# Projections of a decoder trunk: the products of two blocks in one sequence, instead of one block after the other

## The chip, the cores and the metric

The kernel runs on one core of one Trainium2 chip. The metric is the device time of one execution in microseconds. The median of three runs before the change is 2873.17 us, between 2871.62 and 2875.73. One more execution was profiled; its trace is what is read here.

## The reference

The reference is a decoder trunk of two layers (`DEPTH = 2`), with one sequence of 256 tokens, a width of 2048 and 256 memory tokens, all in float32:

```python
def reference(x, mem, ...):
    mem_n = rms_norm(mem, mem_norm_g)
    for l in range(DEPTH):
        hn = rms_norm(x, mix_norm_g[l])
        if l % 2 == 0:
            x = x + even_mixer(hn, ...)      # gated conformer convolution and differential attention
        else:
            x = x + odd_mixer(hn, ...)       # b * causal_conv3(c * u), then a projection
        x = x + cross_attention(rms_norm(x, xattn_norm_g[l]), mem_n, xq_w[l], xk_w[l], xv_w[l], xo_w[l])
        x = x + sq_relu_mlp(rms_norm(x, mlp_norm_g[l]), mlp_w1[l], mlp_w2[l])
    return rms_norm(x, final_norm_g)
```

What matters here are the dense projections with 2048 inputs: `even_w_in` (values and gates of the convolution, q, k, v of 8 differential heads), `even_w_out`, `odd_w_in`, `odd_w_out`, and for each layer `xq`, `xk`, `xv`, `xo` of a cross attention with 4 heads of 512. The convolution of the even layer has 31 taps, and the cross attention's scores are `q k^T / sqrt(512)` with a softmax over the memory.

## The kernel before, in words

**A product in two parts.** Activations lie with channels on the 128 partitions and the 256 tokens along a row. Each float32 number is split into a hi part (rounded to the matmul's fp32r type) and a lo part (what is left). An activation chunk of 128 channels holds hi and lo side by side, 512 columns (`act.both`); `act.hi` is the first half. A block is 128 output channels; its weights are 2048 x 128, loaded as two tiles of 128 x 1024 (eight chunks of inputs each). `weights` (L178) loads one such tile (`raw`), casts it to `whi` on ACT (L189), and makes `wlo` as the difference on DVE (L190). For each of the 16 chunks there is one hi product, 512 columns wide, weights hi times activations hi and lo, and one lo product, 256 columns, weights lo times activations hi. All 32 add up in one PSUM bank of 512 columns (`ps_mm`, four banks), whose halves `summed` (L235) adds: a copy on ACT, an addition on DVE.

**Buffers.** The pools rotate: four `raw` tiles, three `whi` tiles (L71), four `wlo` tiles (L184). A tile is written again when its last reader is done.

**The order of the products.** `proj` (L232, by `proj_group` and `wide_piece`) does a block as 8 hi, 8 lo, 7 hi, 8 lo, 1 hi. `proj_long` (L227) does 15 hi, 16 lo, 1 hi. `proj_rows` (values, rows of tokens) is another form and not touched. `proj` is used for q, k, convolution values and gates, for the keys of layer 0 and the queries of both layers; `proj_long` for the output projections, the input projection of the odd layer and the keys of layer 1.

**What sets the order of other work.** Each call of `weights` first runs what is due by a counter of such calls (L179 to L181): convolution taps from a list, `rate[0]` of them per call (one in the heads, three in the gated channels and behind them), and stages of attention whose delay has passed. In the even layer eight differential heads and eight gated channels alternate in four groups of two heads and two channels; the scores of a head (`sc`, L431) are due two calls after its k block. In cross attention the scores of a head (`sx`, L682) are due one call after its fourth query block (L736), their transposes (`ptx`) one call and the outputs (`pox`) one more behind. Matmuls stand in the order of the program where `strict` is set; loads, `wlo` and taps have orders of their own among themselves; the rest on ACT and DVE is put in order by the scheduler, and each engine then takes its list from the front.

**The MLP** (`Chunk`, `Step`, L760 on), more than half of the span, has its own order and isn't touched.

Of the kernel before, what the change touches and what calls it, by code (L numbers as in the profile page):

```python
# [10 lines left out]
F32 = mybir.dt.float32  # L11
# [3 lines left out]
ALU = mybir.AluOpType  # L15
AX = mybir.AxisListType

P = 128
D = 2048
S = 256  # L20
NC = D // P
# [24 lines left out]
def trunk(ctx: ExitStack, tc: tile.TileContext, d):  # L46
# [184 lines left out]

    def proj(src, act):  # L232
        return proj_group([src], act)[0]

    def summed(ps):  # L235

        t = tmp32("sum")
        A.copy(t, ps[:, S:])
        V.tensor_tensor(t, ps[:, :S], t, op=ALU.add)
        return t  # L240
# [138 lines left out]
    def even_mixer():  # L379
# [40 lines left out]

        def qk(c, hl, name, sign):
            t = summed(proj(w[2 * NA + c], xa))
# [88 lines left out]
        def head(h):  # L511
            mem_piece(m, mss, h)
            if h == H1 - 1:
                stage(4, mem_rows)
            qkt = pools["att"].tile([P, 2, 2, S], F32R, tag="pt", name="dqk")
            q, k = qk(h, qkt[:, 0], "dq", -0.125), qk(H1 + h, qkt[:, 1], "dk", 1.0)
            stage(D0, lambda h=h, q=q, k=k: scores(h, q, k))
# [5 lines left out]
        def gated(c):  # L523
            av = summed(proj(w[c], xa))
            V.tensor_tensor(av, av, r, op=ALU.mult)
            ag = summed(proj(w[NA + c], xa))
            V.tensor_tensor(ag, ag, r, op=ALU.mult)
# [81 lines left out]
        for c, ps in enumerate(proj_group([d["even_out"][c] for c in range(3)], cat, (1, 0))):  # L609
            residual(c, ps, nxt, nss, "xat0")  # L610
        for c in range(3, NC):
            residual(c, proj_long(d["even_out"][c], cat), nxt, nss, "xat0")
        return nxt, nss, kmem


    def odd_mixer(xa, ss):
        w = d["odd_in"]
        y, m = Act(NC, "y"), Act(NC, "mem")
        begun = [NC, 2 * NC, 0, NC + 1]
        made = dict(zip(begun, proj_group([w[c] for c in begun], xa, (1, 0))))  # L620
        r = rstd(ss.acc, D, ss.rows)
        for c in range(NC):
            if c % 2:
                mem_piece(m, None, c // 2)
            cc = summed(made.pop(NC + c) if NC + c in made else proj_long(w[NC + c], xa))
            V.tensor_tensor(cc, cc, r, op=ALU.mult)
            uu = summed(made.pop(2 * NC + c) if 2 * NC + c in made else proj_long(w[2 * NC + c], xa))
            V.tensor_tensor(uu, uu, r, op=ALU.mult)
# [7 lines left out]
            bb = summed(made.pop(c) if c in made else proj_long(w[c], xa))  # L636
            V.tensor_tensor(bb, bb, r, op=ALU.mult)
# [3 lines left out]
        nxt, nss = Act(NC, "xn"), SumSq()  # L641
        for c in range(NC):
            residual(c, proj_long(d["odd_out"][c], y), nxt, nss, "xat1")
        return nxt, nss, kmem
# [31 lines left out]
    def cross(l, xa, ss, kmem):  # L676
# [64 lines left out]
        strict[0] = False  # L741
        for c in range(4, NC):
            residual(c, proj_long(d[f"xo{l}"][c], oa), nxt, nss, f"mlp{l}")
        return nxt, nss
# [488 lines left out]
```

## Time and profile before

| | |
|---|---|
| median of three runs | 2873.17 us |
| profiled execution | 2874.36 us |
| its span, first to last instruction | 2872.2 us |
| mean granted TensorE clock | 0.998 |
| PE busy | 2853.1 us (99%), 15871 matmuls |
| DVE busy | 2258.0 us (79%) |
| ACT busy | 1635.1 us (57%) |
| read from memory | 535.13 MB, 187 GB/s over the span |

How to read it: busy time is what the engine's own instructions took. Matmuls overlap, so a group's sum is more than its time on the engine; the distance from one start to the next is what a matmul costs. In the timeline a row gives the start, the time from the first start to the last end, the engine, the line (most lines are those of helpers: L169 records matmuls, L59 all of ACT and DVE), the operation, out<-in by the program's names, the shapes and the count of instructions merged. A bracket at the end of a row is idle time of that engine just before it, and what ended it. The even layer lies at 0 to 530 us, its cross attention at 530 to 736, its MLP behind it up to 1430; the odd layer's mixer at 1430 to 1965, its cross attention at 1965 to 2170, and the last MLP behind that.

### The profile page before, as it was taken

The numbers are of one execution on the slowest core, as the hardware profiler recorded it, in microseconds if no ns is written. First come the engines' busy times: TensorE is split into PE (matmuls) and PEld (weight loads), VectorE is DVE, ScalarE is ACT, GpSimd is POOL, SyncE is SP. The second block draws the span as 40 slices with busy tenths as digits, with TensorE's granted clock in tenths as the row PEclk, the third lists the DMA queues.
The fourth block names the chain that finished last, engine by engine and source line by source line (L and its number), as shares of the span: only waits on it lengthen the run. The fifth ranks groups of instructions, "written<-read, shape, count | busy, mean of one in ns | idle before, by whom it ended". The sixth has DMA issues, their size and how long they took to land.

```text
span 2872.2 us, 42098 instructions
## 1 busy us (share of the span) xinstructions
PE 2853.1 (99%) x15871; PEld 2484.0 (86%) x15871; DVE 2258.0 (79%) x3489; ACT 1635.1 (57%) x2290; POOL 65.8 (2%) x92
## 2 busy tenths in 40 slices
PE   9999999999999999999999999999999999999998
PEld 7888888898888888888888888888988888888886
DVE  7899987767788888888887765467677888888888
ACT  6665445555565665656654444455555656656565
POOL 0000000000000000000000000000000000000000
PEclk9999999999999999999999999999999999999999
DMA  7455565545686776967666665655456867869675
GB/s 246 159 187 169 183 198 189 171 150 178 199 250 199 219 236 199 265 195 235 192 200 196 196 202 189 194 190 168 152 180 195 252 208 216 232 202 266 191 239 166
DMA packets 210060, 578.27 MB, mean 201 GB/s; under 512 B 17856, under 2 KB 83520, under 8 KB 209856
## 3 DMA queue, kind: packets, MB, share of 16 engines
q1 hardware_dynamic: 199344, 537.30, 57.6%
q0 software_dynamic: 10512, 38.28, 6.8%
q8 instruction: 125, 2.05, 0.3%
q14 instruction: 79, 0.65, 0.1%
HBM read 535.13 MB, written 2.10 MB: 187 GB/s over the span
## 4 chain that ended last, share of the span: by engine, by line
PE 84%; DVE 10%; ACT 3%; DMA 2%; issue 1%; SPq 0%; DVEq 0%; ACTq 0%; POOLq 0%; POOL 0%
PE mm L169 66%; PE p L169 8%; PE mmr L169 7%; DVE wlo L59 3%; DVE cv L59 2%; DVE tw L59 1%; ACT whi L59 1%; DVE raws L59 1%; DVE x L59 1%; PE sx L169 1%; PE pox L169 1%; DMA wlo<-raw 1%; DMA raw<-even_in 1%; DVE sum L59 1%; ACT tw L59 1%
## 5 line engine op out<-in xcount | busy, mean ns | idle before, releaser
L59 ACT CAST whi<-raw 128x1024 fp32r<-128x1024 f32 (+1 forms) x881 | 923.8, 1051 | 465.1 <-PE mm L169 309.5
L59 DVE TENSOR_TENSOR wlo<-raw,whi 128x1024 fp32r<-128x1024 f32 (+1 forms) x808 | 981.8, 1220 | 143.1 <-ACT whi L59 132.7
L169 PE MATMUL mm<-xn,whi 128*128 128x512 f32 x3840 | 938.0, 392 | 0.6 <-DVE xn L59 0.6
L169 PEld LDWEIGHTS mm<-xn,whi 128*128 128x128 f32 x3840 | 702.5, 189 | 133.0 <-DVE xn L59 0.8
L169 PEld LDWEIGHTS mm<-xn,wlo 128*128 128x128 f32 x3840 | 501.2, 191 | 24.0 <-DVE wlo L59 0.2
L169 PE MATMUL mm<-xn,wlo 128*128 128x256 f32 x3840 | 509.5, 283 | 0.0
L59 ACT COPY sum<-mm 128x256 f32<-128x256 f32 x272 | 101.0, 372 | 426.5 <-PE mm L169 424.9
L59 DVE TENSOR_TENSOR sum<-mm,sum 128x256 f32<-128x256 f32 x272 | 114.4, 421 | 183.5 <-ACT sum L59 183.2
L169 PE MATMUL mm<-hid,whi 128*128 128x512 f32 x1024 | 254.9, 391 | 0.0
L169 PEld LDWEIGHTS mm<-hid,whi 128*128 128x128 f32 x1024 | 192.7, 188 | 39.7
L59 ACT CAST tw<-raws 128x1024 fp32r<-128x1024 f32 x128 | 128.5, 1046 | 130.9 <-DVE raws L59 128.8
L59 DVE TENSOR_TENSOR raws<-raws 128x512 f32<-128x512 f32 x256 | 176.5, 689 | 6.0
L59 DVE TENSOR_TENSOR x<-x,mm 128x256 f32<-128x256 f32 x256 | 107.4, 420 | 90.8 <-PE mm L169 86.1
L59 DVE TENSOR_TENSOR tw<-raws,tw 128x1024 fp32r<-128x1024 f32 x128 | 151.8, 1222 | 26.4 <-ACT tw L59 26.2
L169 PE MATMUL p<-tw,hs 128*128 128x512 f32 x576 | 154.3, 394 | 0.7 <-DVE tw L59 0.7
L169 PE MATMUL mmr<-whi,mem 128*128 128x512 f32 x512 | 137.4, 390 | 0.0
L169 PEld LDWEIGHTS mm<-hid,wlo 128*128 128x128 f32 x1024 | 131.0, 191 | 6.4 <-DMA wlo<-raw 1.8
L169 PE MATMUL mm<-hid,wlo 128*128 128x256 f32 x1024 | 133.2, 283 | 0.3 <-DMA wlo<-raw 0.2
L169 PEld LDWEIGHTS p<-tw,hs 128*128 128x128 f32 x576 | 108.1, 188 | 26.3 <-DVE tw L59 1.6
L169 PE MATMUL mm<-mem,whi 128*128 128x512 f32 x512 | 126.3, 393 | 0.0
L169 PE MATMUL mm<-o,whi 128*128 128x512 f32 x512 | 124.7, 392 | 0.0
L786 POOL DMA_DIRECT2D wlo<-raw x73 | 62.1, 852 | 2587.2 <-ACT wlo L59 2213.9
(204 smaller groups left out, 3152.3 us busy)
## 6 DMA issues: line engine op xcount, KB each, us to landing
raw<-w SPq DMA_DIRECT2D x384, 512.0 KB, 4.9
raws<-w SPq DMA_DIRECT2D x128, 512.0 KB, 5.7
raw<-odd_in SPq DMA_DIRECT2D x96, 512.0 KB, 4.6
wlo<-raw POOLq DMA_DIRECT2D x73, 512.0 KB, 7.1
raw<-even_in SPq DMA_DIRECT2D x64, 512.0 KB, 4.5
raw<-xk SPq DMA_DIRECT2D x64, 512.0 KB, 3.7
raw<-xv SPq DMA_DIRECT2D x64, 512.0 KB, 4.1
raw<-xq SPq DMA_DIRECT2D x64, 512.0 KB, 3.8
```

Source lines behind the costliest of these rows:

```text
L59: i = getattr(self.engine, name)(*a, **k)
L169: i = T.matmul(*a, **k)
L786: G.dma_start(out=self.l[g], in_=self.raw[g], accum_op=ALU.add)
```

## The change

A new function, `proj_pair`, makes two blocks together. It takes the weight tiles in the order first half of block 0, first half of block 1, second half of block 0, second half of block 1, and issues 16 hi products (8 per block, of the first 1024 inputs), then all 32 lo products, then the 16 hi products of the other 1024 inputs. It replaces `proj` everywhere, and `proj_long` in pairs of blocks (one block of `even_out` keeps `proj_long`). In the odd layer the 44 blocks of the input projection that follow the first four are made in the order in which they are used, two at a time; a block made early keeps its PSUM bank until it is summed. The four calls of `weights` of a pair now stand: one ahead of the first hi run, one between the two blocks' first hi runs, one ahead of the lo run, and one behind its first eight products.

```diff
@@ -229,8 +229,32 @@
-    def proj(src, act):
-        return proj_group([src], act)[0]
+    def proj_pair(srcs, act):
+        w = [slice(j * P, (j + 1) * P) for j in range(8)]
+        pp = [ps_mm.tile([P, 512], F32, tag="mm", name="mm") for _ in srcs]
+        his, los = [], []
+
+        def lows(i):
+            for j in range(8):
+                mm(pp[i % 2][:, :S], los[i][:, w[j]], act.hi(i // 2 * 8 + j), start=False, stop=False)
+
+        for i in range(4):
+            hi, lo = weights(srcs[i % 2][:, i // 2 * 1024:(i // 2 + 1) * 1024])
+            his.append(hi)
+            los.append(lo)
+            if i < 2:
+                for j in range(8):
+                    mm(pp[i], hi[:, w[j]], act.both(j), start=j == 0, stop=False)
+            else:
+                lows(i - 2)
+        lows(2)
+        lows(3)
+        for i in range(2):
+            for j in range(8):
+                mm(pp[i], his[2 + i][:, w[j]], act.both(8 + j), start=False, stop=j == 7)
+        return pp
...
-            q, k = qk(h, qkt[:, 0], "dq", -0.125), qk(H1 + h, qkt[:, 1], "dk", 1.0)
+            pp = proj_pair([w[2 * NA + h], w[2 * NA + H1 + h]], xa)
+            q, k = qk(pp[0], qkt[:, 0], -0.125), qk(pp[1], qkt[:, 1], 1.0)
...
-            av = summed(proj(w[c], xa))
+            pp = proj_pair([w[c], w[NA + c]], xa)
+            av = summed(pp[0])
             V.tensor_tensor(av, av, r, op=ALU.mult)
-            ag = summed(proj(w[NA + c], xa))
+            ag = summed(pp[1])
...
-        for c in range(3, NC):
-            residual(c, proj_long(d["even_out"][c], cat), nxt, nss, "xat0")
+        residual(3, proj_long(d["even_out"][3], cat), nxt, nss, "xat0")
+        for c in range(4, NC, 2):
+            for i, ps in enumerate(proj_pair([d["even_out"][c + i] for i in range(2)], cat)):
+                residual(c + i, ps, nxt, nss, "xat0")
...
+        order = [n * NC + c for c in range(NC) for n in (1, 2, 0) if n * NC + c not in begun]
+        def block(c):
+            if c not in made:
+                pair, order[:2] = order[:2], []
+                made.update(zip(pair, proj_pair([w[q] for q in pair], xa)))
+            return summed(made.pop(c))
...
-            V.tensor_tensor(keys[c // 8][:, c // 4 % 2, c % 4], summed((proj_long if l else proj)(d[f"xk{l}"][c], m)), mem_r["bc"],
-                            op=ALU.mult)
+            if c % 2 == 0:
+                pp = proj_pair([d[f"xk{l}"][c + i] for i in range(2)], m)
+            V.tensor_tensor(keys[c // 8][:, c // 4 % 2, c % 4], summed(pp[c % 2]), mem_r["bc"], op=ALU.mult)
...
-                s = summed(proj(d[f"xq{l}"][4 * h + i], xa))
+                if i % 2 == 0:
+                    pp = proj_pair([d[f"xq{l}"][4 * h + i + n] for n in range(2)], xa)
+                s = summed(pp[i % 2])
```

Three places of the built program show what moves. The first is TensorE at the second head of the first cross attention: `sx` are the 24 products of the head's scores, all other rows are projection products. Before:

```order
L169 MATMUL mm<-xn,whi 128x512 x9
L169 MATMUL mm<-xn,wlo 128x256 x8
L169 MATMUL mm<-xn,whi 128x512 x7
L169 MATMUL mm<-xn,wlo 128x256 x8
L169 MATMUL mm<-xn,whi 128x512 x9
L169 MATMUL mm<-xn,wlo 128x256 x8
L169 MATMUL sx<-hl,xq 128x256 x24
```

In the changed program:

```order
L169 MATMUL mm<-xn,whi 128x512 x16
L169 MATMUL mm<-xn,wlo 128x256 x32
L169 MATMUL mm<-xn,whi 128x512 x24
L169 MATMUL sx<-hl,xq 128x256 x24
L169 MATMUL mm<-xn,whi 128x512 x8
```

The scores stood behind 8 hi and 8 lo products of the next block (the ninth hi product of the row above belongs to the block before); now they stand behind the 8 hi products of the next pair, of the 24 in the row above.

The second place is ACT and DVE at the same scores (`xq_5832` is the head's query, `sum_6123` the sum of its fourth block, the numbers behind `whi` and `wlo` go up in the order of loading). ACT before:

```order
L59 COPY sum_6069<-mm_5992 128x256
L59 CAST whi_6132<-raw_6131 128x1024
L59 CAST xq_5832<-sum_6069 128x256
L59 CAST whi_6203<-raw_6202 128x1024
L59 COPY sum_6123<-mm_6078 128x256
L59 CAST whi_6232<-raw_6231 128x1024
L59 CAST xq_5832<-sum_6123 128x256
L59 CAST whi_6262<-raw_6261 128x1024
```

ACT in the changed program:

```order
L59 COPY sum_6114<-mm_5992 128x256
L59 CAST whi_6196<-raw_6195 128x1024
L59 CAST xq_5832<-sum_6114 128x256
L59 COPY sum_6123<-mm_5993 128x256
L59 CAST whi_6210<-raw_6209 128x1024
L59 CAST whi_6232<-raw_6231 128x1024
L59 CAST xq_5832<-sum_6123 128x256
```

DVE in the changed program:

```order
L59 TENSOR_TENSOR sum_6114<-sum_6114,rb_5716 128x256
L59 TENSOR_TENSOR wlo_6197<-raw_6195,whi_6196 128x1024
L59 TENSOR_TENSOR xq_5832<-sum_6114,xq_5832 128x256
L59 TENSOR_TENSOR sum_6123<-mm_5993,sum_6123 128x256
L59 TENSOR_TENSOR wlo_6211<-raw_6209,whi_6210 128x1024
L59 TENSOR_TENSOR sum_6123<-sum_6123,rb_5716 128x256
L59 TENSOR_TENSOR wlo_6233<-raw_6231,whi_6232 128x1024
L59 TENSOR_TENSOR xq_5832<-sum_6123,xq_5832 128x256
```

Between the copy of the fourth block's sum and the cast of the query stood one cast of a hi tile; now two stand there, those of the third and fourth tile of the next pair (`whi_6210`, `whi_6232`), and on DVE their two lo tiles.

The third place is TensorE at the last gated channel of the second group (`po` is the end of a head's output, `nmr` a mean). Before:

```order
L169 MATMUL mm<-xn,whi 128x512 x7
L169 MATMUL mm<-xn,wlo 128x256 x8
L169 MATMUL mm<-xn,whi 128x512 x9
L169 MATMUL mm<-xn,wlo 128x256 x8
L169 MATMUL nmr<-onec_105,osq 128x1 x2
L169 MATMUL mm<-xn,whi 128x512 x7
L169 MATMUL mm<-xn,wlo 128x256 x8
L169 MATMUL mm<-xn,whi 128x512 x9
```

In the changed program:

```order
L169 MATMUL mm<-xn,whi 128x512 x8
L169 MATMUL mm<-xn,wlo 128x256 x8
L169 MATMUL po<-ahl,vh 128x256
L169 MATMUL po<-ahl,vl 128x256
L169 MATMUL po<-ahl,vh 128x256 x2
L169 MATMUL po<-ahl,vl 128x256
L169 MATMUL po<-ahl,vh 128x256
L169 MATMUL mm<-xn,wlo 128x256 x24
L169 MATMUL mm<-xn,whi 128x512 x24
```

A block ended with eight lo products and one hi product; the pair ends with its last lo products and sixteen hi products (the other eight of the 24 belong to the next pair).

More of the change, by code (lines that the diff above doesn't have):

```diff
@@ L419, in even_mixer, with qk @@
         orig = half.tile([P, H1, S], F32, tag="half", name="orig")
-        def qk(c, hl, name, sign):
-            t = summed(proj(w[2 * NA + c], xa))
+        def qk(ps, hl, sign):
+            t = summed(ps)
             V.scalar_tensor_tensor(t, t, sign, r, op0=ALU.mult, op1=ALU.mult)
@@ L624, in odd_mixer @@
                 mem_piece(m, None, c // 2)
-            cc = summed(made.pop(NC + c) if NC + c in made else proj_long(w[NC + c], xa))
+            cc = block(NC + c)
             V.tensor_tensor(cc, cc, r, op=ALU.mult)
-            uu = summed(made.pop(2 * NC + c) if 2 * NC + c in made else proj_long(w[2 * NC + c], xa))
+            uu = block(2 * NC + c)
             V.tensor_tensor(uu, uu, r, op=ALU.mult)
@@ L635, in odd_mixer @@
                                        op0=ALU.mult, op1=ALU.add)
-            bb = summed(made.pop(c) if c in made else proj_long(w[c], xa))
+            bb = block(c)
             V.tensor_tensor(bb, bb, r, op=ALU.mult)
@@ L641, in odd_mixer @@
         nxt, nss = Act(NC, "xn"), SumSq()
-        for c in range(NC):
-            residual(c, proj_long(d["odd_out"][c], y), nxt, nss, "xat1")
+        for c in range(0, NC, 2):
+            for i, ps in enumerate(proj_pair([d["odd_out"][c + i] for i in range(2)], y)):
+                residual(c + i, ps, nxt, nss, "xat1")
         return nxt, nss, kmem
@@ L741, in cross @@
         strict[0] = False
-        for c in range(4, NC):
-            residual(c, proj_long(d[f"xo{l}"][c], oa), nxt, nss, f"mlp{l}")
+        for c in range(4, NC, 2):
+            for i, ps in enumerate(proj_pair([d[f"xo{l}"][c + i] for i in range(2)], oa)):
+                residual(c + i, ps, nxt, nss, f"mlp{l}")
         return nxt, nss
```

## The prediction

> **What bounds the kernel now.** First the page: busy time, the chain that ended last, and the groups.
>
> ```profile
> span 2872.2 us, 42098 instructions
> PE 2853.1 (99%) x15871; PEld 2484.0 (86%) x15871; DVE 2258.0 (79%) x3489; ACT 1635.1 (57%) x2290; POOL 65.8 (2%) x92
> PE 84%; DVE 10%; ACT 3%; DMA 2%; issue 1%; SPq 0%; DVEq 0%; ACTq 0%; POOLq 0%; POOL 0%
> L59 ACT CAST whi<-raw 128x1024 fp32r<-128x1024 f32 (+1 forms) x881 | 923.8, 1051 | 465.1 <-PE mm L169 309.5
> L59 DVE TENSOR_TENSOR wlo<-raw,whi 128x1024 fp32r<-128x1024 f32 (+1 forms) x808 | 981.8, 1220 | 143.1 <-ACT whi L59 132.7
> L59 DVE TENSOR_TENSOR sum<-mm,sum 128x256 f32<-128x256 f32 x272 | 114.4, 421 | 183.5 <-ACT sum L59 183.2
> ```
>
> TensorE works 99% of the span, so anything is won only by fewer or closer matmuls, and every wait put in front of a matmul is paid in full. The cast of a hi tile takes 1.05 us on ACT (it mostly waits for matmuls to free a buffer), the lo tile 1.22 us on DVE, a 256-wide DVE step 0.42 us.
>
> Second the timeline of TensorE, for what a switch between hi and lo products costs. First one block in the form of proj_long (one hi run and one lo run), then one in the form of proj (two of each):
>
> ```profile
> 464.16 0.40 PE L169 MATMUL mm<-co,whi 128*128 128x512 f32 x1
> 464.39 2.00 PE L169 MATMUL mm<-ca,whi 128*128 128x512 f32 x8
> 466.23 1.75 PE L169 MATMUL mm<-co,whi 128*128 128x512 f32 x7
> 467.82 1.12 PE L169 MATMUL mm<-ca,wlo 128*128 128x256 f32 x8
> 468.77 1.12 PE L169 MATMUL mm<-co,wlo 128*128 128x256 f32 x8
> 469.73 0.40 PE L169 MATMUL mm<-co,whi 128*128 128x512 f32 x1
> ```
> ```profile
> 207.78 2.23 PE L169 MATMUL mm<-xn,whi 128*128 128x512 f32 x9
> 209.84 1.12 PE L169 MATMUL mm<-xn,wlo 128*128 128x256 f32 x8
> 210.80 1.78 PE L169 MATMUL mm<-xn,whi 128*128 128x512 f32 x7
> 212.41 1.12 PE L169 MATMUL mm<-xn,wlo 128*128 128x256 f32 x8
> 213.36 2.23 PE L169 MATMUL mm<-xn,whi 128*128 128x512 f32 x9
> ```
>
> A block takes 469.73 - 464.16 = 5.57 us with one round hi-lo-hi and 213.36 - 207.78 = 5.58 us with two. A hi product takes (467.82 - 464.16)/16 = 0.229 us, a lo product (469.73 - 467.82)/16 = 0.119 us. A switch is almost free already.
>
> Third the busy time by stretch (columns: PE, PEld, DVE, ACT, POOL, each with its count, clock, DMA share, GB/s), for what is near its limit beside TensorE: the two gated channels of the third group, the two heads of the fourth, the keys of layer 0, and the queries of layer 0:
>
> ```profile
> 178.00:204.00 26.00, 26.00 (x165) 22.84 (x164) 25.57 (x64) 17.32 (x37) 0.63 (x2) 1.00 0.43 135
> 204.00:228.00 24.00, 24.00 (x148) 21.06 (x148) 21.88 (x55) 15.99 (x31) 0.00 (x0) 1.00 0.69 227
> 254.00:345.00 91.00, 89.94 (x514) 76.26 (x513) 89.57 (x182) 42.70 (x63) 0.00 (x0) 1.00 0.55 177
> 536.00:650.00 114.00, 113.92 (x718) 102.93 (x718) 81.62 (x132) 63.82 (x100) 0.00 (x0) 1.00 0.48 156
> ```
>
> VectorE is busy 98% in the gated channels and the keys (25.57 of 26, 89.57 of 91), 91% in the heads and 72% in the queries. So in the even layer lo tiles are made with hardly any lead.
>
> **The change part by part.** *Products and loads* stay: 192 blocks of 32 matmuls, the same casts and transfers, 0 us.
>
> *Switches.* 80 blocks lose two rounds each (q, k, gates, keys of layer 0, queries) and 112 one: 272 rounds become one per pair, 96. 176 rounds less x (5.58 - 5.57 = 0.01 us) = -1.8 us; with rounding between 0 and -3.5.
> The Trainium skill, "TensorE: Matmul & The Clock Gate", section Back-to-back issue gap, speaks against any gain here: the gap hangs on the width alone, N/2.4 + 2.5 ns. By that -1.8 would be 0 and the sum 1.8 us more. The rows lie over its 216 and 109 ns, and one round's 0.01 us is at their resolution.
>
> *Hi buffers.* A pair holds four hi tiles, the pool has three. Let T be the end of a pair on TensorE, the next pair's hi tiles h0 to h3. From the order of use: h1 takes the buffer that the old third hi tile frees at T-1.83 (8 x 0.229), h2 the one freed at T, and h3 the one that h0 frees at T+1.83. Needed are they at T+1.83 (h1), T+7.5 and T+9.3, so the products themselves don't wait: h1 is cast by T-0.35 (sum copy 0.37, cast 1.05), 2.2 us ahead. 0 us.
>
> *The scores of cross attention* are what is late next. They stay queued one weights call after the head's fourth query. That call came in the middle of a block, it now stands ahead of the second hi run, at T+1.83. The chain they wait for, before:
>
> ```profile
> 549.08 0.37 ACT L59 COPY sum<-mm 128x256 f32<-128x256 f32 x1 [2.56 <-PE mm L169]
> 549.35 1.05 ACT L59 CAST whi<-raw 128x1024 fp32r<-128x1024 f32 x1
> 549.49 0.42 DVE L59 TENSOR_TENSOR sum<-mm,sum 128x256 f32<-128x256 f32 x1 [1.71 <-ACT sum L59]
> 549.95 0.43 DVE L59 TENSOR_TENSOR sum<-sum,rb 128x256 f32<-128x256 f32 x1
> 550.41 0.41 ACT L59 CAST xq<-sum 128x256 fp32r<-128x256 f32 x1
> 550.43 1.23 DVE L59 TENSOR_TENSOR wlo<-raw,whi 128x1024 fp32r<-128x1024 f32 x1
> 551.58 0.42 DVE L59 TENSOR_TENSOR xq<-sum,xq 128x256 fp32r<-128x256 f32 x1
> 551.67 3.04 PE L169 MATMUL sx<-hl,xq 128*128 128x256 f32 x24
> 554.55 1.78 PE L169 MATMUL mm<-xn,whi 128*128 128x512 f32 x7
> ```
>
> The query's lo half starts at 551.58, behind a wlo, though its hi half was there at 550.82: an engine takes its queue in order. It ends 2.95 us after the block (552.00 against 549.05), and only the 11th score product needs it, 10 x 0.12 us (24 in 2.88) after 551.67: no wait. In the new order the last query's cast stands on ACT behind h3's, and on DVE its lo half stands behind the lo tile of h3. h3 can't be cast before T+1.83, and ends at T+2.93. DVE meanwhile: lo of h1 from T-0.3 to +0.85, the third query's lo half, the sum to +1.6, lo of h2 to +2.75, the scaling to +3.1, lo of h3 to +4.25, the query to T+4.7 (steps at their spacing of 1.15 and about 0.34 to 0.42). The 11th score product is due at T+1.83+1.20 = T+3.03, so TensorE stands still for **1.7 us**. For the fourth head the scores stand behind a hi and a lo run of the output projection, due at T+4.0: 0.7 us. Per layer 3 x 1.7 + 0.7 = 5.8, for two layers **+11.5 us**. From below: the old chain of 2.95 us would just fit under 3.03, 0. From above: one cast and one lo tile more in the queues (2.27) makes 4.0 per head, 27. I take the queue's own sum, since each step is a row above.
>
> *The lo tiles of the even layer.* Their last tile was the one with one hi product (0.23) left to do after its run; in a pair sixteen are left (3.67). So VectorE must have it 3.44 us earlier, measured from the end of the pair. The sum and scaling of the first block (2 x 0.34) now stand behind it, which leaves 2.76. What lead is there at the end of the gated channels of groups two and three:
>
> ```profile
> 149.15 1.22 DVE L59 TENSOR_TENSOR wlo<-raw,whi 128x1024 fp32r<-128x1024 f32 x1
> ```
> ```profile
> 150.96 1.11 PE L169 MATMUL mm<-xn,wlo 128*128 128x256 f32 x8
> ```
> ```profile
> 198.76 0.42 DVE L59 TENSOR_TENSOR sum<-sum,rb 128x256 f32<-128x256 f32 x1
> 199.10 0.42 DVE L59 TENSOR_TENSOR lsum<-lsum,cv 128x256 f32<-128x256 f32 x1
> 199.43 1.22 DVE L59 TENSOR_TENSOR wlo<-raw,whi 128x1024 fp32r<-128x1024 f32 x1
> ```
> ```profile
> 200.74 1.18 PE L169 MATMUL mm<-xn,wlo 128*128 128x256 f32 x8
> 299.51 1.22 PE L169 MATMUL mm<-mem,wlo 128*128 128x256 f32 x8 [0.48 <-DVE wlo L59]
> ```
>
> 150.96 - 150.37 = 0.59 us, 200.74 - 200.65 = 0.09 us, and in the keys none: TensorE waits there already. So group two loses 2.76 - 0.59 = 2.2, group three 2.7, and group four with the keys, one stretch in which VectorE never catches up, about 2.5 once (the values behind it give a little back). Group one has no convolution taps yet: 0. Together **+7.4 us**. Part of it will show as a wait of the differential scores, which now stand at T+3.64 behind the k block's lo half; it is the same lateness. From below 0, if VectorE starts each stretch further ahead than before; from above 3.44 for each of three and 1.3 more for the second head of each: 14.
>
> *The row statistics of cross attention* are transposed six microseconds after their mean instead of four and a half:
>
> ```profile
> 536.05 0.28 PE L169 MATMUL mm<-xn,wlo 128*128 128x256 f32 x1
> 536.40 0.41 PE L174 MATMUL nmb<-ident,rrow 128*128 128x128 f32 x2
> ```
>
> 0.35 against 0.12 us is a wait of 0.23, gone in both layers: -0.5 us.
>
> *Even_out, odd_in, odd_out, xo and the keys of layer 1*: TensorE's instructions there are hi and lo runs alone; DVE per pair needs 4 x 1.15 and some eight steps of 0.34 to 0.42, 8 of 11.1 us. 0 us.
>
> Sum: -1.8 + 11.5 + 7.4 - 0.5 = +16.6 us. The profiled execution took 2874.36 us for its 2872.2 of span, 1.2 over the median of 2873.17, so 2874.4 + 16.6 = 2891.0 stands for a median of about **2890 us**.
>
> **The rivals.** *Only the cross scores wait* (the even layer hides the earlier tiles, since the first lo tile of a pair is needed 1.8 us later than before): 2873.2 - 2.3 + 11.5 = 2882. For it: 91% in the heads leaves 2 us a pair to get ahead. Against: 98% in the gated channels.
>
> *It is faster.* The place is the keys of layer 0, where 0.48 us is waited at 299.51: sixteen hi products stand ahead of the first lo run instead of eight, which gives VectorE's tile 1.83 us more. If that ends the keys' waits (about 3 us in 254 to 345, where PE is idle 91.00 - 89.94 = 1.1 and the rest hides in the modelled ends) and the scores' chain stays at its 2.95 us, the time is 2873.2 - 1.8 - 0.5 - 3 = 2868. It decides when the query's cast goes ahead of h3's. Against: that order is written in the queues.
>
> *No change*: waits of 2 us that cancel 2 us of switches, 2873. It needs both large terms at their lower ends.
>
> *Three hi buffers bind in every pair*: should ACT reach h1 over 2.2 us late, each of 96 pairs would wait; at 0.2 us each 2890 + 19 = 2909. ACT is busy 57%, but softmax comes in bursts.
>
> **How the numbers follow.** What a measurement of this kernel can tell from no change is about 0.2%, 5.7 us. Chances: the forecast 0.55, only cross 0.2, every pair 0.1, no change 0.08, faster 0.07. Slower by over 0.2% is the first three with their low ends taken off: 0.84; within 0.2% 0.10; faster 0.06. The forecast's own range is 2884 to 2898. The range of 8 in 10 takes in the cross-only case with half of its price (2873.2 - 2.3 + 7 = 2878) and, above, both upper terms in part (2890 + 4.5 + 10 = 2904).
>
> **What would show it.** Right: a wait of 1.5 to 2 us inside each of the first three groups of 24 sx per layer, released by DVE xq, and 0.5 to 1 in the fourth; waits of 2 to 3 us per group at sc or lo runs in 128 to 254, released by DVE dqk or wlo; blocks of 11.13 us per pair elsewhere. Wrong: sx running through in 2.9 us, or hi runs that wait for ACT whi in the odd layer.

## The result, and the profile after

The changed kernel takes 2901.35 us (median, 2899.5 to 2901.84) against 2873.68 us for the kernel before in the same session: **27.7 us slower, a ratio of 1.0095 with a 95% interval of 1.0083 to 1.0107**. The prediction was 2890, in a range of 2878 to 2904. The profiled execution took 2899.5 us, with a span of 2897.7 us, 25.5 over that of before; the stretches below are those of the two profiled executions and add up to 25.5, not to 27.7.

The page of the changed kernel, span, busy time and groups:

```profile
span 2897.7 us, 42078 instructions
PE 2860.5 (99%) x15871; PEld 2489.6 (86%) x15871; DVE 2241.6 (77%) x3489; ACT 1636.5 (56%) x2290; POOL 66.1 (2%) x92
L59 ACT CAST whi<-raw 128x1024 fp32r<-128x1024 f32 (+1 forms) x881 | 924.1, 1052 | 479.8 <-PE mm L169 327.7
L59 DVE TENSOR_TENSOR wlo<-raw,whi 128x1024 fp32r<-128x1024 f32 (+1 forms) x808 | 981.4, 1221 | 142.8 <-ACT whi L59 133.1
```

The engines' work is the same: 15871 matmuls, 881 casts, 808 lo tiles, at the same durations (the 20 instructions fewer in the span's row are none of the engines' busy ones). What is new shows in what TensorE waits for. Its waits before (engine, line, what it waited for, us in total, times, longest):

```profile
PE nmb L174 <- DVE rrow L59: 2.9, 2, 2.6
PE mm L169 <- DVE wlo L59: 0.9, 3, 0.5
```

And in the changed kernel:

```profile
PE sx L169 <- DVE xq L59: 7.6, 10, 1.0
PE po L169 <- DVE ahl L59: 3.9, 6, 0.8
PE nmb L174 <- DVE rrow L59: 3.3, 4, 2.6
PE sx L169 <- ACT xq L59: 2.8, 6, 0.6
PE mm L169 <- DVE wlo L59: 2.7, 5, 0.7
...
PE sc L169 <- DVE dqk L59: 1.3, 4, 0.6
...
PE nmb L174 <- DVE mrcol L59: 0.8, 1, 0.8
```

The cross scores (`sx`) that the prediction named head the list, but second stands a wait it did not have: the head outputs of the even layer (`po`), for `ahl`. This view undercounts, since the ends of matmuls are modelled; so where the time went is read from the starts. A stretch is the time from TensorE's first product on one kind of input to its first on the next:

| stretch | before | after | difference |
|---|---|---|---|
| heads and gated channels (layer 0) | 199.4 | 209.9 | +10.5 |
| keys of layer 0 | 94.8 | 95.8 | +1.0 |
| queries of layer 0, with the scores of three heads | 108.8 | 116.7 | +8.0 |
| output projection of layer 0, with the fourth head's | 95.6 | 96.4 | +0.8 |
| queries of layer 1 | 108.8 | 115.2 | +6.5 |
| output projection of layer 1 | 95.6 | 96.4 | +0.8 |
| all the rest (MLPs, odd layer, even_out, values, start) | 2169.3 | 2167.3 | -2.0 |

In the heads and gated channels the starts of the products, less 0.227 us for a hi and 0.120 for a lo product, divide the 10.5 us: 6.4 ahead of or behind `po`, 3.6 inside the groups of `sc`, 1.0 at the memory's row statistics, 1.1 in the lo runs, and -1.6 between hi products, of which there are fewer runs.

The timeline at the head outputs of the second gated channel, group two. Before, the transposes `ptd` and the six `po`:

```profile
142.30 0.49 PE L174 MATMUL ptd<-ident,pexp 128*128 128x128 f32 x3
...
148.65 0.28 PE L169 MATMUL po<-ahl,vh 128*128 128x256 f32 x1
148.77 0.28 PE L169 MATMUL po<-ahl,vl 128*128 128x256 f32 x1
148.89 0.40 PE L169 MATMUL po<-ahl,vh 128*128 128x256 f32 x2
```

After, TensorE and, below it, ACT:

```profile
143.12 0.49 PE L174 MATMUL ptd<-ident,pexp 128*128 128x128 f32 x3
...
146.67 0.33 PE L169 MATMUL po<-ahl,vh 128*128 128x256 f32 x1
146.84 0.28 PE L169 MATMUL po<-ahl,vl 128*128 128x256 f32 x1
147.87 0.75 PE L169 MATMUL po<-ahl,vh 128*128 128x256 f32 x2 [0.75 <-DVE ahl L59]
148.46 0.28 PE L169 MATMUL po<-ahl,vl 128*128 128x256 f32 x1
149.41 0.39 PE L169 MATMUL po<-ahl,vh 128*128 128x256 f32 x1 [0.67 <-DVE ahl L59]
```
```profile
143.54 1.04 ACT L59 CAST whi<-raw 128x1024 fp32r<-128x1024 f32 x1
144.59 1.28 ACT L59 ACT_TABLE_LOAD   x1
145.88 0.42 ACT L59 ACTIVATE sum<-sum 128x256 f32<-128x256 f32 x1
146.21 0.36 ACT L59 CAST ahl<-ptd 128x256 fp32r<-128x256 f32 x1
```

Between transposes and outputs lay 148.65 - 142.30 = 6.35 us; now it is 146.67 - 143.12 = 3.55. In both kernels they are two calls of the weights function apart. A cast of a hi tile, a table load and a sigmoid, which in this trace stand on ACT ahead of `ahl`, alone take 2.7 us (143.54 to 146.21).

### The profile page after: what moved, and what is told of

It reads as the page before. It is cut to its first block, busy times and chain, and to the rows that moved or that the text cites. A ratio compares the mean times of both kernels' runs of the same rounds, so it can differ in the third digit from the quotient of the medians.

```text
span 2897.7 us, 42078 instructions
## 1 busy us (share of the span) xinstructions
PE 2860.5 (99%) x15871; PEld 2489.6 (86%) x15871; DVE 2241.6 (77%) x3489; ACT 1636.5 (56%) x2290; POOL 66.1 (2%) x92
## 4 chain that ended last, share of the span: by engine, by line
PE 87%; DVE 8%; ACT 2%; issue 2%; DMA 1%; SPq 0%; DVEq 0%; ACTq 0%; POOLq 0%; POOL 0%
PE mm L169 69%; PE p L169 8%; PE mmr L169 7%; DVE wlo L59 2%; DVE tw L59 1%; DVE cv L59 1%; ACT whi L59 1%; PE pox L169 1%; DVE x L59 1%; DVE raws L59 1%; PE sx L169 1%; DVE sum L59 0%; DVE slo L59 0%; ACT tw L59 0%; DMA wlo<-raw 0%
## 5 line engine op out<-in xcount | busy, mean ns | idle before, releaser
L169 PE MATMUL mm<-xn,whi 128*128 128x512 f32 x3840 | 917.1, 391 | 0.6 <-DVE xn L59 0.6
L169 PEld LDWEIGHTS mm<-xn,wlo 128*128 128x128 f32 x3840 | 486.1, 191 | 15.2
L169 PE MATMUL mm<-xn,wlo 128*128 128x256 f32 x3840 | 494.5, 283 | 0.0
```

What stands on the lines that cost most here:

```text
L169: i = T.matmul(*a, **k)
```

## The experiments

The times in the second column are medians; the text under each edit is what was expected before that kernel ran. The other columns are the stretches of one profiled execution each in us, as in the table above (h+g: heads and gated channels; q, xo: queries and output projections of a layer):

| kernel | median | ratio to before (95%) | h+g | keys 0 | q 0 | xo 0 | q 1 | xo 1 |
|---|---|---|---|---|---|---|---|---|
| before | 2873 | 1 | 199.4 | 94.8 | 108.8 | 95.6 | 108.8 | 95.6 |
| the change | 2901.35 | 1.0095 (1.0083-1.0107) | 209.9 | 95.8 | 116.7 | 96.4 | 115.2 | 96.4 |
| q_single | 2886.99 | 1.0048 (1.0033-1.0063) | 212.0 | 95.8 | 108.8 | 95.5 | 108.8 | 95.5 |
| even_single | 2889.05 | 1.0056 (1.0040-1.0073) | 199.3 | 94.7 | 115.2 | 96.4 | 115.2 | 96.4 |
| both_single | 2871.85 | 0.9996 (0.9987-1.0006) | 199.3 | 93.8 | 108.8 | 95.5 | 108.8 | 95.5 |
| po_later | 2894.02 | 1.0074 (1.0059-1.0089) | 205.7 | 95.6 | 115.2 | 96.4 | 116.6 | 96.4 |
| sx_later | 2898.59 | 1.0087 (1.0072-1.0102) | 210.1 | 95.8 | 113.9 | 96.4 | 113.9 | 96.4 |
| q_order | 2895.75 | 1.0078 (1.0061-1.0095) | 212.8 | 95.8 | 111.6 | 97.3 | 111.7 | 97.3 |
| all_later | 2892.30 | 1.0067 (1.0052-1.0082) | 205.5 | 95.8 | 113.9 | 96.4 | 113.9 | 96.4 |
| few_taps | 2898.98 | 1.0088 (1.0073-1.0103) | 209.4 | 96.3 | 116.6 | 96.4 | 115.2 | 96.4 |
| even_ticks | 2886.07 | 1.0047 (1.0032-1.0062) | 203.9 | 96.0 | 112.6 | 96.4 | 112.6 | 96.4 |
| even_ticks_x | 2881.39 | 1.0029 (1.0018-1.0041) | 203.9 | 96.0 | 110.0 | 96.4 | 110.0 | 96.4 |
| ticks_rates | 2876.97 | 1.0013 (1.0003-1.0022) | 199.2 | 96.0 | 110.1 | 96.4 | 110.1 | 96.4 |
| ticks_few | 2871.53 | 0.9994 (0.9985-1.0003) | 199.2 | 91.3 | 110.1 | 96.4 | 110.0 | 96.4 |

### Undoing one part at a time

`q_single` (`proj` stands in it as before):

```diff
-                if i % 2 == 0:
-                    pp = proj_pair([d[f"xq{l}"][4 * h + i + n] for n in range(2)], xa)
-                s = summed(pp[i % 2])
+                s = summed(proj(d[f"xq{l}"][4 * h + i], xa))
```

> The changed kernel with one part undone: the queries of both cross attentions (128 blocks' halves, 32 blocks) are again made one block at a time, hi-lo-hi-lo, everything else stays in pairs. By stretch of TensorE's own products the change made the queries 8.0 us longer in layer 0 and 6.5 in layer 1, and the output projections behind them 0.8 each, which hold the fourth head's scores. Theory (the scores became due before their last query is ready): all of it comes back, 2901.4 - 16.1 = 2885, and no score product waits over 0.1 us for DVE xq. Prediction's own size of that term: 2901.4 - 11.5 = 2890. Rival (VectorE is late on entry, from the even layer, and stays late whatever the form of the queries): the waits stay, 2898 to 2901.

`even_single`:

```diff
-            pp = proj_pair([w[2 * NA + h], w[2 * NA + H1 + h]], xa)
+            q = qk(proj(w[2 * NA + h], xa), qkt[:, 0], -0.125)
+            k = qk(proj(w[2 * NA + H1 + h], xa), qkt[:, 1], 1.0)
...
-            pp = proj_pair([w[c], w[NA + c]], xa)
-            av = summed(pp[0])
+            av = summed(proj(w[c], xa))
...
-            ag = summed(pp[1])
+            ag = summed(proj(w[NA + c], xa))
...
+            if l == 0:
+                ps = proj(d[f"xk{l}"][c], m)
...
```

> The changed kernel with another part undone: heads, gated channels and keys of layer 0 are again made one block at a time; queries and all later projections stay in pairs. By stretch the change made heads and gated channels 10.5 us longer, the keys 1.0, the values behind them 0.5 shorter. Theory (the loss lies in these stretches and nowhere else): 2901.4 - 11.0 = 2890. The prediction's size of the term (lo tiles alone): 2901.4 - 7.4 = 2894. Rival (VectorE hands its lateness on, so that the queries' loss shrinks too when it starts rested): under 2886.

`both_single` holds both edits.

> Both parts undone: pairs are left only in even_out, the input and output projections of the odd layer, the keys of layer 1 and the output projections of the cross attentions (112 blocks that were made in one long hi run and one long lo run). Theory (a pair by itself costs nothing, the switches that it saves are 56 rounds at 0.01 us): 2873.7 - 0.6 = 2873, not to be told from the kernel before. Rival (three hi buffers for four tiles cost 0.1 to 0.2 us a pair here too): 56 pairs, 2879 to 2885. Rival (the losses of the two parts aren't additive): over 2878.

Measured: 2887.0, 2889.1 and 2871.9, where the theory had 2885, 2890 and 2873. Queries and output projections fall back to 108.8 and 95.5 us, the even layer to 199.3; each part gives its loss back alone. The two gains, 14.4 and 12.3, add up to 26.7; both together gave 29.5, more rather than less. So the loss lies in the stretches where other work (attention, and the convolution's taps on VectorE) stands between the blocks, and pairs as such cost nothing measurable: with 112 blocks left in pairs the kernel is level with before (0.9996, 0.9987 to 1.0006). For these pairs the rival with three hi buffers is ruled out by it.

### Moving single products back

`po_later` gives the head outputs one call more (`D2` is that delay):

```diff
-    D0, D1, D2, D3 = 2, 3, 2, 2
+    D0, D1, D2, D3 = 2, 3, 3, 2
```

> The changed kernel with one number changed: the six products of a differential head's output (po) are due three calls of the weights function behind the transposes instead of two, that is ahead of the next pair instead of inside the lo run of the second gated channel. They wait there for DVE ahl, some 2 us in groups two and three and 1.6 in group four, 5.7 in all. Theory (the products came due too early; the tile they need is late only for them): these waits go and nothing takes their place, 2901.4 - 5.7 = 2896. Rival (VectorE, 98% busy, is the bound of the gated channels; while po waits it makes the lo tiles that the next lo run needs): the wait moves to the lo runs of mm and the scores behind, 2900 to 2902.

2894.0 us, a little better than the theory's 2896, but not for its reason. The waits at `po` are gone from the view, and heads and gated channels win 4.2 of the 10.5 us. Something did take their place, as the rival had it: waits for `wlo` went from 2.7 us in 5 to 3.8 in 8, and by the starts the lo runs of this stretch lost 3.1 us where the change lost 0.6. The stretches don't show where the rest of the 7.3 us between the medians comes from.

```profile
PE sx L169 <- DVE xq L59: 7.6, 10, 1.0
PE mm L169 <- DVE wlo L59: 3.8, 8, 1.2
```

`sx_later` gives the cross scores of three heads one call more:

```diff
-            stage(X0, lambda h=h, q=q, k=k: scores(h, q, k))
+            stage(2 if h < XH - 1 else X0, lambda h=h, q=q, k=k: scores(h, q, k))
```

> The changed kernel with the cross scores of the first three heads due two calls of the weights function behind the fourth query instead of one: they stand ahead of the pair's lo run, 1.83 us later on TensorE, with all else where it was. Theory (only the place of the scores is wrong: the query's lo half is there 4.7 us after the pair's end, the eleventh product would be due at 4.86): the waits of these three heads go, 6.4 of the 7.4 us per layer, 12.5 to 14.5 us in all with the half clock of the profiled execution, 2901.4 - 13 = 2888; the fourth head keeps its 0.8. Rival (the queues of ACT and DVE are late by more than the place, so that the wait only moves to the later scores or to the lo run behind them): half of it stays, 2895.

2898.6 us: a miss by ten. The second and third head's scores ran through (the first head's still lost 1.0 us), and 1.3 us a head were lost again at the outputs, which the expectation had not followed. The timeline of the second head:

```profile
604.18 0.60 PE L174 MATMUL ptx<-ident,pexp 128*128 128x128 f32 x4
604.53 2.10 PE L169 MATMUL mm<-xn,whi 128*128 128x512 f32 x8
606.47 0.39 PE L169 MATMUL pox<-pb,hl 128*128 128x256 f32 x2
607.95 2.87 PE L169 MATMUL pox<-pb,hl 128*128 128x256 f32 x22 [1.08 <-DVE pb L59]
```

The transposes are due two calls behind the scores (`X1 = 2`; the description of the kernel before says one). Moved by one call, they fall on the next pair's first call, and the outputs, one call behind, on its second: eight hi products, 1.83 us, where the change had 6.5 and the kernel before 2.8. The same delay in calls had become another time.

`q_order` leaves the scores where the change put them and takes the query past the lo tiles on DVE (`ordered` keeps instructions of one label in the program's order; the lo tiles have it already):

```diff
-                V.tensor_tensor(s, s, r, op=ALU.mult)
+                steps = [V.tensor_tensor(s, s, r, op=ALU.mult)]
                 A.copy(q[:, 0, i], s)
-                V.tensor_tensor(q[:, 1, i], s, f(q[:, 0, i]), op=ALU.subtract)
+                steps.append(V.tensor_tensor(q[:, 1, i], s, f(q[:, 0, i]), op=ALU.subtract))
+                if i > 1:
+                    for n in steps:
+                        ordered(n, "lo")
```

> The changed kernel with the scores where the change put them, but with the scaling and the lo half of each head's third and fourth query held in the program's order among the lo tiles on DVE: they stand ahead of the next pair's four lo tiles instead of behind the last of them. (The transposes of the row statistics move eight lo products earlier with it.) Theory (the query waits in DVE's queue behind lo tiles that nobody needs yet): the fourth query is ready about 3 us after the pair's end, the scores run through in 2.9 us, and the lo tiles come in time behind it, 2901.4 - 14 = 2887, perhaps 1 more for the row statistics. Rival (the casts on ACT are the bound, DVE's order doesn't matter): at most a quarter of it goes, 2898. Rival (the lo tiles, now 3 us later, are late instead): waits in front of mm with wlo, 2890 to 2896.

2895.8 us. All scores run through, which shows that the order of VectorE's queue was the cause and not the hi buffers; but the softmax, now behind the lo tiles, is late for the transposes, and at the fourth head the lo tiles themselves are late, as the second rival had it. DVE at the second head's scores, then TensorE:

```profile
593.96 0.43 DVE L59 TENSOR_TENSOR xq<-sum,xq 128x256 fp32r<-128x256 f32 x1 [0.47 <-ACT xq L59]
594.30 2.35 DVE L59 TENSOR_TENSOR wlo<-raw,whi 128x1024 fp32r<-128x1024 f32 x2
```
```profile
593.81 3.04 PE L169 MATMUL sx<-hl,xq 128*128 128x256 f32 x24
...
600.18 0.81 PE L174 MATMUL ptx<-ident,pexp 128*128 128x128 f32 x4 [0.54 <-DVE pinv L59]
```

`all_later` has the edits of `po_later` and `sx_later`, and the differential scores one call later, their transposes where they were:

```diff
-    D0, D1, D2, D3 = 2, 3, 2, 2
+    D0, D1, D2, D3 = 3, 2, 3, 2
```

> The changed kernel with every wait's place moved back: cross scores of the first three heads one call later, differential scores one call later (eight lo products), head outputs one call later, transposes where they were. Theory (places alone): cross 13 us and head outputs 5.7 and scores 1.9 to 3.6 go, of which VectorE's own lateness in the gated channels and keys gives 1.5 back as in the kernel with later head outputs: 2901.4 - 13 - 5.7 - 2.5 + 1.5 = 2882. Rival (VectorE is the bound from 128 to 345 us, and each place that is moved back shows as a wait of a lo run): 2888, as with the cross scores alone. To beat the kernel before, 2873.6, it would have to win 28 us; by neither theory it does.

2892.3 us: neither theory; the gains of the two kernels about add up, and the later differential scores bring nothing (205.5 against 205.7 us). What they win, 2.1 us inside the groups of `sc` by the starts, is lost again at the memory's row statistics (2.1 us against 1.0) and in the lo runs (4.0 against 3.1). Moving one product back at a time moves much of the wait to the next.

### Is it the place or VectorE's load?

`few_taps` takes work from VectorE and moves no projection product or head output in this stretch. It leaves 15 of the 31 taps of the convolution out, so its output is not the reference's:

```diff
-    R1, R2, R3 = 1, 3, 3
+    R1, R2, R3 = 1, 1, 3
...
-            for j in range(CK - 1, -1, -1):
+            for j in range(CK - 1, CK // 2 - 1, -1):
```

> The changed kernel with 16 of the 31 convolution taps left out of the computation's end (15 are not computed), and one tap per call of the weights function in the gated channels instead of three: VectorE has 16 steps of 0.46 us fewer per group there, 7.4 of 26 us. Its output isn't the reference's. Places of all products stay. Theory (VectorE's load makes scores and head outputs late): heads and gated channels fall from 209.9 to about 201 us, the keys' waits of 4.8 us go, 2901.4 - 9 - 4 = 2888. Rival (the place alone: 2.8 us between a head's transposes and its products, with a table load and a hi tile's cast on ACT between them, are too few whatever VectorE does): the head outputs keep 4 to 6 us, 205 to 208 us, 2893 to 2896.

2899.0 us, nearer to the rival: h+g falls by only 0.5. This execution has 1.5 us at half clock in that stretch (202.3 to 205.7 us, last section); without it h+g would have fallen by 2.0, of which the starts put 1.3 at `sc` and 0.9 at `po`. VectorE's busy time in 128 to 152 us falls from 23.72 to 19.93 of 24 (first columns of a stretch: PE, PEld, DVE), first the change, then `few_taps`:

```profile
128.00:152.00 24.00, 22.33 (x141) 19.24 (x140) 23.72 (x61) 16.48 (x34) 0.72 (x2) 1.00 0.44 141
```
```profile
128.00:152.00 24.00, 22.55 (x145) 19.56 (x144) 19.93 (x50) 16.79 (x35) 0.62 (x2) 1.00 0.49 158
```

and the outputs wait in the same places all the same, `few_taps`:

```profile
147.58 0.75 PE L169 MATMUL po<-ahl,vh 128*128 128x256 f32 x2 [0.80 <-DVE ahl L59]
...
149.09 0.39 PE L169 MATMUL po<-ahl,vh 128*128 128x256 f32 x1 [0.65 <-DVE ahl L59]
```

So it is mainly the place that makes them wait: 5.5 of the 6.4 us at `po` and 2.3 of the 3.6 at `sc` stay with VectorE's load a sixth lower. On the keys the kernel tells nothing: at three taps a call they stayed as full as before (43.98 of 45 us in 300 to 345), which its expectation overlooked.

### Spacing the stages evenly

`even_ticks` keeps every projection product and load in the change's order, looks for due stages at four evenly spaced points of a pair (`tick`) and counts their delays in these points:

```diff
-    def weights(src):
+    def weights(src, own=True):
         run_later(rate[0], calls[0])
-        run_stages(calls[0])
+        if own:
+            tick()
...
+        tick()
         for i in range(4):
...
+                    if i == 1 and j == 4:
+                        tick()
...
+        tick()
         lows(2)
...
+                if i == 0 and j == 4:
+                    tick()
```

> The changed kernel, products and loads in the same order, but the stages of attention are looked at at evenly spaced points of a pair instead of at its four calls of the weights function: ahead of the pair, after 12 hi products, after 16 lo products, after 4 of the last 16 hi products (each 2.75 to 2.9 us apart, as the calls stood before the change; the calls themselves are 1.83, 1.83, 0.95 and 6.5 us apart). All delays keep their numbers. Theory (the waits come from the uneven spacing: a delay of so many calls is now less time than the chain behind it needs): head outputs and differential scores run through, heads and gated channels fall from 209.9 to 202 us; cross scores are due at 2.75 us behind the pair instead of 1.83, so 0.9 to 1 us less per head for three heads and two layers, 5.7, and the half clock of the profiled execution, 1.5, goes with the waits: 2901.4 - 8 - 6 = 2887. Rival (VectorE or the casts of the pairs' tiles are the bound, spacing doesn't matter): the waits move to the lo runs or to the scores behind, 2896 to 2901.

`even_ticks_x` adds the edit of `sx_later`.

> The same with the cross scores of the first three heads due two of these points behind the fourth query instead of one, 5.6 us behind its pair. Theory (as above; in the kernel with later scores the wait went to the outputs because only 1.83 us lay between them and the transposes, here 2.75 do as in the kernel before): score and output products of these heads run through, the fourth head keeps 0.8 us: queries 110 us a layer instead of 115.3 to 116.7, 2901.4 - 8 - 12 = 2881. Rival (the wait again goes to the outputs): 3.7 us a layer come back, 2888. What is left to the 2873.6 of the kernel before would be the fourth heads (1.6), the memory row statistics and the keys of layer 0 (2), the row statistics (0.4).

2886.1 and 2881.4 us, where the theory had 2887 and 2881 (h+g falls to 203.9, though, not to 202). The waits at `po`, `sc` and the memory's row statistics are gone in both; in `even_ticks_x` three heads' scores run through, with 0.4 us a head (by the starts) left at the outputs. The waits of `even_ticks_x`:

```profile
PE mm L175 <- DVE wlo L59: 6.5, 11, 0.8
...
PE sx L175 <- DVE xq L59: 1.3, 2, 0.6
...
PE pox L175 <- DVE pb L59: 1.0, 6, 0.2
```

What is left are the fourth heads and the lo tiles: in the change VectorE went on making lo tiles while `po` waited; now the lo runs of heads and gated channels wait (5.7 us by their starts against 0.6 in the change). Group two:

```profile
134.12 1.22 PE L175 MATMUL mm<-xn,wlo 128*128 128x256 f32 x8 [0.54 <-DVE wlo L59]
...
147.55 1.22 PE L175 MATMUL mm<-xn,wlo 128*128 128x256 f32 x8 [0.56 <-DVE wlo L59]
```

This is the term that the prediction had seen, h+g 203.9 - 199.4 = 4.5 us. Two last kernels ask whether it is VectorE's load. `ticks_rates` computes everything and spreads the taps evenly over heads and gated channels:

```diff
-    R1, R2, R3 = 1, 3, 3
+    R1, R2, R3 = 2, 2, 3
```

> The kernel with evenly spaced stages and later cross scores, and two convolution taps per call of the weights function in heads and gated channels alike, instead of one in the heads and three in the gated channels: the same number per group, but 8 of 24 taps (0.46 us each) leave each pair of gated channels, where VectorE is busy 97 to 99%, for the heads, where it is busy 87 to 92%. Theory (what is left in the even layer are lo tiles that VectorE finishes late, because it has no spare time in the gated channels): the lo runs' waits in heads and gated channels, about 4.5 us, fall to under 1.5, the keys keep theirs; 2881.4 - 3 = 2878. Rival (the last lo tile of a pair is late by the order of use, whatever VectorE's load): no change, 2881. Rival (the taps now delay the heads' scores): waits at sc, 2882 to 2885.

`ticks_few` leaves 15 taps out as `few_taps` does, with `R1, R2, R3 = 1, 1, 2`.

> The same kernel with evenly spaced stages and later cross scores, 15 of the 31 taps of each channel not computed, one tap per call in heads and gated channels and two in the keys. Its output isn't the reference's. VectorE has 16 steps of 0.46 us fewer in each pair of gated channels and about 32 fewer in the keys. Theory (VectorE's load makes the lo tiles late, once the places are right): the waits of the lo runs go in both stretches, heads and gated channels 203.9 to 199.5, keys 96.0 to about 93, 2881.4 - 7 = 2874. Rival (order of use): they stay, 2879 to 2881.

2877.0 and 2871.5 us, both a little below the theories' 2878 and 2874. With the taps spread, heads and gated channels are back at 199.2 us, and the lo run of the same gated channel is one run again:

```profile
143.29 4.00 PE L175 MATMUL mm<-xn,wlo 128*128 128x256 f32 x32
```

With taps missing in the keys too, these fall from 96.0 to 91.3 us, and no wait for `wlo` is left in them. Once the places are right, both waits are thus VectorE's load; in heads and gated channels only how it is spread, since `ticks_rates` computes every tap.

No complete version is faster than the kernel before: the best one with pairs everywhere, `ticks_rates`, is still 0.13% over before (0.03 to 0.22), and `both_single` can't be told from it.

## Why the prediction was right, and where it was not

**Sign and range** were right: slower, 2901.4 in 2878 to 2904. The size was 27.7 us where it said 16.6. That this still lies in the range is in part luck: the range's upper end was made of larger sizes of the two terms, while some 6 us came from the head outputs, which were in no term, and from the differential scores, beyond what late lo tiles explain, and 1.5 from a stretch at half clock. Of the two signs that it gave, the one at the cross scores held. The other, waits of 2 to 3 us per group at `sc` or lo runs, did not: by the starts these lost 3.6 and 1.1 us in all, and `po`, which it does not name, 6.4. Step by step:

- *Switches*, -1.8 us. The rest of the program, in which no new wait of this size shows, became 2.0 us shorter, though the start of the program alone differs by up to 2 us between executions (the first head starts at 52.5 and 53.0 us in these two, at 54.3 and 54.7 in two others). In odd_in, xk1 and odd_out, 271.2 to 270.7, 89.1 to 88.9 and 89.1 to 88.9, it is 0.8 us for 76 blocks, or 0.02 us a round. The size for the whole kernel can't be settled closer: `both_single` is 0.04% below before, inside its interval.
- *Hi buffers*, 0. Right. The view of waits names no `whi` for `mm`, and 112 blocks in pairs cost nothing.
- *Cross scores*, +11.5. The mechanism was right, wait and place alike; the term was mis-sized, 16.1 us by the stretches (8.0 + 6.5 + two of 0.8). The second and third head lost 1.85 us each against 1.7, the fourth 0.89 against 0.7. The first lost 2.7: there the third query was late too, its lo half at 562.66, and by the trace DVE split the head's keys and values (`hl`) inside this very pair, ahead of it; in the second head it did so at 581.6 and 583.7, ten us ahead. No run moves that work alone. And 1.5 us in layer 0 are no wait at all (last section). The size from above, 27, doesn't follow from its own 4.0 us a head, which gives 25 to 30 with the fourth heads; the sum doesn't use it. The prediction applied one working to all three heads. The second head's rows, the lo tile of h3 on DVE and the wait behind it:

```profile
595.15 1.23 DVE L59 TENSOR_TENSOR wlo<-raw,whi 128x1024 fp32r<-128x1024 f32 x1
```
```profile
596.76 1.94 PE L169 MATMUL sx<-hl,xq 128*128 128x256 f32 x14 [0.76 <-DVE xq L59]
```

The first head's, DVE and then TensorE:

```profile
558.25 1.22 DVE L59 TENSOR_TENSOR hl<-vals,hl 128x1024 fp32r<-128x1024 f32 x1
...
562.66 0.42 DVE L59 TENSOR_TENSOR xq<-sum,xq 128x256 fp32r<-128x256 f32 x1
```
```profile
561.11 1.05 PE L169 MATMUL sx<-hl,xq 128*128 128x256 f32 x7
563.13 0.50 PE L169 MATMUL sx<-hl,xq 128*128 128x256 f32 x2 [0.98 <-DVE xq L59]
563.90 0.39 PE L169 MATMUL sx<-hl,xq 128*128 128x256 f32 x1 [0.27 <-ACT xq L59]
564.94 3.07 PE L169 MATMUL sx<-hl,xq 128*128 128x256 f32 x14 [0.65 <-DVE xq L59]
```

- *Lo tiles of the even layer*, +7.4. This step failed, in two ways. The stretch lost 11.5 us, of which only about half is what the step described: 4.5 us in heads and gated channels, which even spacing lays bare (203.9) and spreading the taps takes away (199.2), and 1.0 in the keys, a size no larger than the spread of that stretch among three programs alike there (93.8 to 94.8). The other 6.0 us is the uneven spacing of the calls (209.9 to 203.9). The prediction used that spacing for the cross scores, whose place it followed from T+0 to T+1.83, and not for the head outputs; its third place of the order even showed `po` moved from the end of a block into the lo run. It also guessed that the differential scores' wait would be "the same lateness": with even spacing they run through while lo tiles are late; only 1.3 of their 3.6 us went with the load in `few_taps`.
- *Row statistics*, -0.5. Wrong in sign. By the starts two waits of 0.2 us became 0.4 each. With the query's steps ahead of the lo tiles, in `q_order`, they are 0.3; with single queries, in `q_single`, 0.3 too. Why DVE's chain for them comes later was not isolated.
- *Only cross* (2882) and *faster* (2868) are ruled out by `q_single` and `even_single`, where each part alone is slower than before; *every pair* (2909) by `both_single`, though its time came nearer than those two and than the forecast's own 2890. *No change* (2873) needed both large terms at their lower ends; their stretches lost 16.1 and 11.5 us.
- *Switch gaps by the Trainium skill*, "TensorE: Matmul & The Clock Gate", section Back-to-back issue gap. Row and rule differ by 1.8 us in 2873. The section gives the formula for an isolated matmul; for a stream with weight loads it has about 131 ns at 512 columns, and the rows here, with 227 to 229 ns, agree with neither figure. The 0.02 us a round above speaks for the row, but the whole kernels don't settle it.

## What to carry to other kernels

Where delays are counted in steps of the program, a change that regroups the steps changes every delay in time: list the new distance in microseconds of each producer and consumer, not only of those at the place that you look at. A delay moved by one step moves those chained to it as well, and a wait removed at one place takes away the time in which a loaded engine caught up, so the next wait shows only then. TensorE, busy 99%, was slowed by several chains that hid one another: undo by parts first, then by causes.

## What the runs showed of the hardware

Behind the first head's waits in layer 0 the score products stood 0.21 us apart for a while instead of 0.12. The busy time by stretch gives the granted clock (third number from the end), first of the change, then of `q_order` behind the head outputs of group three:

```profile
560.00:564.00 4.00, 2.75 (x16) 2.15 (x14) 4.00 (x7) 2.71 (x5) 0.00 (x0) 1.00 0.43 135
564.00:566.00 2.00, 1.35 (x7) 1.15 (x8) 1.37 (x4) 1.15 (x1) 0.00 (x0) 0.83 0.80 240
566.00:568.60 2.60, 2.60 (x12) 2.47 (x12) 0.62 (x4) 0.57 (x2) 0.00 (x0) 0.50 0.56 208
```
```profile
205.00:208.20 3.20, 3.20 (x17) 3.20 (x16) 1.98 (x4) 0.92 (x3) 0.00 (x0) 0.50 0.84 196
```

The clock fell to a half from 565.3 to 568.7, for 3.4 us, which cost 1.5 us on top of the waits (116.7 us against 115.2 for the queries of layer 1), and it was back while TensorE ran on. The waits did not bring it each time: in layer 1 the same waits, to 0.02 us, were followed by full clock in this execution. Over the fourteen profiled executions, waits that add up to 2.0 us or more inside 4 us occurred 19 times, and 7 of these were followed by such a stretch; of the 21 with 1.6 to 1.8 us none was. So h+g took 209.9, 212.0 and 212.8 us in programs that are alike there, with none, one and two such stretches of about 1.5 us loss each. The Trainium skill, "TensorE: Matmul & The Clock Gate", section What's actually happening, has the clock halved behind at least one idle window of about 3.4 us and restored by one busy window. The length of the stretch, 3.4 us, agrees; but here no single gap was over 1.2 us where the clock fell, and several short ones close together went ahead of it.
